# A hybrid decoder block on one core: the first query tile of the a heads in one matmul, the first weights cast by two engines, and fewer low parts on GpSimd

## The chip, the core and the metric

The kernel runs on one core of a Trainium2 chip. The metric is the device time of one execution in microseconds (us), less is better. Each time below is either the median of separate runs or comes from one profiled execution. The engines are named as in the profile: PE is TensorE's matmul stream and PEld its weight loads, DVE is VectorE, ACT is ScalarE, POOL is GpSimd, SP is the queue from which nearly all DMAs are issued.

## What is computed

The reference is one layer of a decoder block on 512 tokens of width 2048, in float32:

```python
h = _rms_norm(x, norm1_g[l])
proj = h @ w_in[l]
aq, ak, av, bu, bg, cq, ck, cv = jnp.split(proj, splits, axis=-1)
...
out_a = _dilated_mixture(aq, ak, av)        # 8 heads x 64, three dilated windows
out_b = _conformer_conv(bu, bg, ...)        # GLU, causal conv of 31 taps, LayerNorm, swish
out_c, _ = _band_attention(cq, ck, cv, C_WINDOW - 1, sinks=c_sinks[l])   # 16 heads, window 128
mix = jnp.concatenate([out_a, out_b, out_c], axis=-1)
x = x + mix @ w_out[l]
h2 = _rms_norm(x, norm2_g[l])
x = x + (jax.nn.silu(h2 @ w_gate[l]) * (h2 @ w_up[l])) @ w_down[l]
```

## The kernel before

**Precision.** Every float32 operand is held as a high part (`fp32r`, made by a cast on ACT) and a low part (what is left, made by a subtraction). A product is three matmuls: high with high, high with low, low with high. Helper `mm3` issues them (lines L312 to L314).

**Weights.** All weights come as units of 128x1024 numbers. `next_unit` hands the next one to PE, and ahead of that `split_up_to` splits units to come: `wh` is the high part, `wl` the low part. For the units of the input and output projections ACT casts (L289) and DVE subtracts (L290), both in SBUF. From a point behind the output projection on, ACT casts twice, once into a PSUM tile `wn` ("near") and once into SBUF (L293, L294), and DVE subtracts the PSUM copy (L295). That point is the number `len(units) + 4`: units 0 to 3 of the feed-forward part are still split in SBUF, and unit 4, called ('12', 'g1') in the profile, is the first with a near copy. Besides, POOL adds pairs of these units (L200), which the feed-forward part's seven products per block (as in Strassen's scheme) need.

**Stages.** First the head: `x` arrives in 16 tiles, each is scaled by the norm's weights (high part on ACT at L419, low part on DVE at L420) and multiplied for four column groups at once into the banks `in0` to `in3`; here the tokens are the stationary operand and 512 weights stream. Then `project` makes the other 26 column groups one by one, with attention work between their matmuls. Then come the output projection (banks `o`, L312 to L314 again), the gate and up projections (L1125, banks `out`) and the down projection (L1267, L1125).

**Order.** There is no scheduler on the chip: a table of "ticks" sets at which point in PE's stream each step of attention is recorded, and each engine executes its own list in that order, waiting on semaphores.

**Attention.** `attention` handles two heads at a time. `scores` multiplies one tile of 128 queries with the keys; the query holds its high part in 64 partitions and its low part in the other 64, so one matmul with the keys' high part `kh` and one with their low part `kl` give the whole product. `top` takes the row maximum with the mask added, `exps` the exponential, `norm` the sum and POOL's multiplication by its inverse (L779). `flip` transposes the weights on PE into a bank `t` (L795), ACT and DVE split them (`ph`, `pl`), and `weigh` multiplies by the values (bank `o`, L819 and L820). For the c heads the first query tile has 128 keys only; their high and low parts stand beside each other in a tile `k0`, one matmul of 256 columns meets both (L736), and `top` adds the two halves with a copy on ACT and an add on DVE (tile `kl`, L746 and L747). The a heads have two matmuls of 128 columns there (L738 and L739).

**Rows of the mix.** Each finished pair of heads is a row (`c0`, `a2`, ...) of the output projection's input. `split_mix` splits it: `mh` by ACT (L864), `ml` by POOL for c rows and by DVE for the others (L865). The output projection starts with `first_two`, which multiplies rows in the order c0, c1, c2, c4, c5, c3, c7, c6 for two column groups; `split_rows(k)` splits the rows from k on that are due.

Of the kernel before, what the change touches and what calls it, by code (L numbers as in the profile page):

```python
# [9 lines left out]
F32 = mybir.dt.float32  # L10
F32R = mybir.dt.float32r
# [4 lines left out]
P = 128  # L16
T = 512
NT = T // P
D = 2048
KT = D // P  # L20
# [28 lines left out]
ROWS = "c0 c1 c2 c4 c5 c3 c7 c6 a0 a1 b2 b1 b0 b3 a2 a3".split()  # L49
# [38 lines left out]
C_G1, C_G2, C_CW, C_CB, C_LG, C_LB, C_QK, C_SINK, C_ALL = 0, 16, 32, 156, 160, 164, 168, 172, 188  # L88
# [34 lines left out]
def kernel(ctx: ExitStack, tc: tile.TileContext, xT, wi, wo, wgu, wd, cst_in, outT):  # L123
    nc = tc.nc
# [20 lines left out]
    def slot(name, dt=F32, cols=T):  # L145
        return sp.tile([P, cols], dt, name=name, tag="s")
# [19 lines left out]
    raws, held = {}, {}  # L166
# [101 lines left out]
    splits = {}  # L268
# [11 lines left out]
    def split_up_to(i):  # L280
        while at["split"] <= min(i, len(works) - 1):
            key, last, eng = works[at["split"]]
            t, n = drop(key) if last else raws[key]
            u = at["split"]
            hi = wp.tile([P, 1024], F32R, name=f"wh{u}", tag="hi", bufs=SPLIT_BUFS)
            lo = wp.tile([P, 1024], F32R, name=f"wl{u}", tag="lo", bufs=SPLIT_BUFS)
            if eng or u < len(units) + 4:
                eng = eng or nc.vector
                nc.scalar.copy(hi[:, :n], t[:, :n])  # L289
                eng.tensor_sub(lo[:, :n], t[:, :n], hi[:, :n].bitcast(F32))  # L290
            else:
                near = psum["high"].tile([P, 1024], F32R, name=f"wn{u}", tag="h")
                nc.scalar.copy(near[:, :n], t[:, :n])  # L293
                nc.scalar.copy(hi[:, :n], t[:, :n])  # L294
                nc.vector.tensor_sub(lo[:, :n], t[:, :n], near[:, :n].bitcast(F32))  # L295
            splits[u] = (hi, lo)
            at["split"] += 1
# [13 lines left out]
    def mm3(out, wh, wl, xh, xl, start, stop):  # L311
        nc.tensor.matmul(out, wh, xh, start=start, stop=False)  # L312
        nc.tensor.matmul(out, wh, xl, start=False, stop=False)  # L313
        nc.tensor.matmul(out, wl, xh, start=False, stop=stop)  # L314
# [4 lines left out]
    xs = []  # L319
# [27 lines left out]
    def col(i):  # L347
        return cst[:, i:i + 1]
# [64 lines left out]
    def scaled(x, g, tag, k):  # L413
        if k < N_WIDE:
            both = wide(k, f"{tag}{k}", F32R)
            hi, lo = both[:, :T], both[:, T:]
        else:
            hi, lo = slot(f"{tag}h{k}", F32R), slot(f"{tag}l{k}", F32R)
        nc.scalar.activation(hi, x, AF.Copy, scale=g)  # L419
        nc.vector.scalar_tensor_tensor(lo, x, g, hi.bitcast(F32), op0=ALU.mult, op1=ALU.subtract)  # L420
        return hi, lo
# [19 lines left out]

    g4 = [(column if j < COLUMN_BANKS - 1 else bank)(f"in{j}") for j in range(HEAD4)]
    h_hl = {}
    for k in range(2):
        h_hl[k] = scaled(xs[k], col(C_G1 + k), "h", k)
        split_up_to(k)
    pump(RAW_EARLY)
    add_square(ssum, xs[0], 0, "sq")
    for k in range(KT):
        if k + 2 < KT:  # L450
            h_hl[k + 2] = scaled(xs[k + 2], col(C_G1 + k + 2), "h", k + 2)
        if k < 2 or k % 2 == 0:
            wh, wl = next_unit()
            o = 0
        if k + X_AHEAD < KT:
            load_first(k + X_AHEAD)
        if k == 4:
            nc.sync.dma_start(cst[:, C_G2:], cst_in[:, C_G2:])
        if k + 1 < KT:
            add_square(ssum, xs[k + 1], k + 1, "sq")  # L460
        hi, lo = h_hl.pop(k)
        h_hi.append(hi)
        h_lo.append(lo)
        for i in range(NT):
            s = slice(i * P, (i + 1) * P)
            mm3(g4[i], hi[:, s], lo[:, s], wh[:, o:o + T], wl[:, o:o + T], k == 0, k == KT - 1)
        o += T
    xs = None
    c64 = cp.tile([P, NT], F32, name="c64")
# [142 lines left out]
    def do_k(box, b, name, gi):  # L612
        def then(r):
            ticks.after(2, widen, r)

        raw = head_scales(b, name, then)
        box["k at"] = ticks.now + SQ + TD + 10
        both = []

        def widen(r):  # L620
            wide = slot(name + "wide")
            nc.scalar.copy(wide.rearrange("p (a b c) -> p a b c", a=NT, b=2),
                           r[:, :, :, None].to_broadcast([P, NT, 2, HD]))
            ticks.after(1, flip, wide)

        def flip(wide):
            b2 = bank(name + "t")
            for i in range(NT):
                nc.tensor.transpose(b2[:, i * P:(i + 1) * P], wide[:, i * P:(i + 1) * P], ident)
            ticks.after(1, scale, b2)  # L630

        def scale(b2):
            for h in range(2):
                both.append(slot(f"{name}{h}"))
                nc.vector.scalar_tensor_tensor(both[h][HALF[h]], raw[HALF[h]], gqk[HALF[h], gi:gi + 1], b2[HALF[h]],
                                               op0=ALU.mult, op1=ALU.mult)
            ticks.after(1, twin)

        def twin():
            for h in range(2):  # L640
                nc.sync.dma_start(both[h][HALF[1 - h]], both[h][HALF[h]])
            ticks.after(TD, high)

        def high():
            box["k"] = [(slot(f"{name}h{h}", F32R), slot(f"{name}l{h}", F32R)) for h in range(2)]
            for h in range(2):
                nc.scalar.copy(box["k"][h][0], both[h])
            ticks.after(1, low)

        def low():  # L650
            for h, (hi, lo) in enumerate(box["k"]):
                nc.vector.tensor_sub(lo, both[h], hi.bitcast(F32))
            if gi == 1:
                box["k0"] = [slot(f"{name}0{h}", F32R, 2 * P) for h in range(2)]
                for k0, src in zip(box["k0"], both):
                    nc.scalar.copy(k0[:, :P], src[:, :P])
                    nc.vector.tensor_sub(k0[:, P:], src[:, :P], k0[:, :P].bitcast(F32))
# [21 lines left out]
    def do_v(box, b, name):  # L679
# [22 lines left out]

    UNITS = {
        "c": [[(0, 0, 128, 0), (1, 0, 256, 256)], [(2, 128, 256, 0), (3, 256, 256, 256)]],
        "a": [[(0, 0, 128, 0), (1, 0, 256, 128)], [(2, 0, 384, 0)], [(3, 0, 512, 0)]],
    }

    TBANKS = {
# [6 lines left out]
    def attention(kind, box, mix, mi, heads):  # L715
# [7 lines left out]
        def head(h):  # L723
# [5 lines left out]
            def scores(u):  # L729
                q = box["q"][h]  # L730
                kh, kl = box["k"][h]
                b = banks[u] = bank(f"{name}s{h}{u}")
                for i, k0, n, o in us[u]:
                    qs, ks = slice(i * P, (i + 1) * P), slice(k0, k0 + n)
                    if kind == "c" and i == 0:
                        nc.tensor.matmul(b[:, o:o + 2 * n], q[:, qs], box["k0"][h], start=True, stop=True)  # L736
                        continue
                    nc.tensor.matmul(b[:, o:o + n], q[:, qs], kh[:, ks], start=True, stop=False)  # L738
                    nc.tensor.matmul(b[:, o:o + n], q[:, qs], kl[:, ks], start=False, stop=True)  # L739

            def top(u):
                b, rq = banks[u], box["rq"]
                s = slice(us[u][0][0], us[u][-1][0] + 1)
                if kind == "c" and u == 0:
                    with_kl = slot(f"kl{h}", F32, P)
                    nc.scalar.copy(with_kl, b[:, P:2 * P])  # L746
                    nc.vector.tensor_add(with_kl, with_kl, mask[:, mw - P:])  # L747
                for i, k0, n, o in reversed(us[u]):
                    other = with_kl if kind == "c" and i == 0 else mask[:, mw - n:]
                    nc.vector.tensor_tensor_reduce(b[:, o:o + n], b[:, o:o + n], other,  # L750
                                                   op0=ALU.add, op1=ALU.max, scale=1.0, scalar=-3.0e38,
                                                   accum_out=mx[:, i:i + 1])
                nc.vector.scalar_tensor_tensor(nm[:, s], mx[:, s], -1.0, rq[:, s, h], op0=ALU.mult, op1=ALU.mult)
                if kind == "c":
                    nc.vector.tensor_scalar(nm[:, s], nm[:, s], nsink[:, heads[h]:heads[h] + 1], None, op0=ALU.min)
# [104 lines left out]
    def split_mix(name):  # L860
        if name not in m_hi:
            m = mix.pop(name)
            hi, lo = slot(f"mh_{name}", F32R), slot(f"ml_{name}", F32R)
            nc.scalar.copy(hi, m)  # L864
            (nc.gpsimd if name[0] == "c" else nc.vector).tensor_sub(lo, m, hi.bitcast(F32))  # L865
            m_hi[name], m_lo[name] = hi, lo

    vd = tc.dram_tile([NT, P, T], F32, name="vd")
# [136 lines left out]
            operand(q, j, src)  # L1005

    def split_rows(k):
        for name in ROWS[k:k + 3]:
            if name in mix:
                split_mix(name)  # L1010

# [524 lines left out]
```

## Time and profile before

| what | value |
|---|---|
| median of 3 runs | 1879.63 us (1879.41 to 1881.6) |
| profiled execution, its own time | 1879.36 us |
| its span, first to last instruction | 1877.5 us |
| granted TensorE clock, mean over the span | 1.00 |
| busy share of PE, DVE, ACT, POOL | 100%, 77%, 72%, 65% |
| instructions of PE | 9848 matmuls, 9848 weight loads |

A row of the timeline reads: start in us, duration in us, engine, line of the kernel, operation, tile written, tiles read, shapes, count; in brackets the idle time of the engine before it and what ended that. A busy PE is not PE at its peak: matmuls overlap, and a matmul of 512 columns that is shown with 0.39 us starts 0.23 us after the one before it. So the cost of a matmul is read from start to start.

### The profile page before, as it was taken

How to read it: one execution, taken by the hardware profiler on the slowest of the kernel's cores; microseconds unless marked ns; L12 is line 12 of the kernel's file. 1: busy time of each engine (PE TensorE's matmuls, PEld its weight loads, DVE VectorE, ACT ScalarE, POOL GpSimd, SP SyncE). 2: the span in 40 equal slices, each digit the busy share in tenths (PEclk: the TensorE clock that was granted, in tenths of full speed). 3: DMA queues.
4: the chain of work that ended last, by engine and by line, in shares of the span. 5: the costliest groups of instructions: out<-in, count | busy, mean ns of one | idle time of the engine just before them, and what ended most of it. 6: DMA issues, size and time to landing. Idle time of an engine off the chain costs nothing.

```text
span 1877.5 us, 28557 instructions
## 1 busy us (share of the span) xinstructions
PE 1871.7 (100%) x9848; PEld 1609.1 (86%) x9848; DVE 1454.1 (77%) x2376; ACT 1343.7 (72%) x1883; POOL 1217.0 (65%) x812
## 2 busy tenths in 40 slices
PE   9999999999999999999999999999999999999999
PEld 7888888888888888888888888888888888888888
DVE  7578999897679777777777777777777677778887
ACT  6246655553466887888878888888888887777675
POOL 5023444362155887778878877888787767766786
PEclk9999999999999999999999999999999999999999
DMA  7333233333342354443544445344455475578984
GB/s 271 122 109 102 81 105 102 121 107 138 113 146 89 114 178 142 163 163 132 184 134 164 162 137 181 132 166 160 145 175 196 151 237 185 196 253 283 311 241 124
DMA packets 157986, 301.09 MB, mean 160 GB/s; under 512 B 29968, under 2 KB 69008, under 8 KB 157840
## 3 DMA queue, kind: packets, MB, share of 16 engines
q1 hardware_dynamic: 157696, 299.25, 48.8%
q8 instruction: 78, 1.28, 0.3%
q14 instruction: 68, 0.56, 0.1%
q10 hardware_dynamic: 144, 0.01, 0.0%
HBM read 241.27 MB, written 50.33 MB: 155 GB/s over the span
## 4 chain that ended last, share of the span: by engine, by line
PE 96%; DVE 1%; issue 1%; ACT 1%; POOL 1%; DMA 0%; SPq 0%; DVEq 0%; POOLq 0%; ACTq 0%
PE out L1125 51%; PE out L1267 16%; PE o L313 3%; PE o L314 3%; PE o L312 3%; PE cq L312 1%; PE cq L313 1%; PE cq L314 1%; PE in L313 1%; PE ak L312 1%; PE bg L312 1%; PE ak L314 1%; PE ak L313 1%; PE bu L312 1%; PE bu L314 1%; PE bg L313 1%
## 5 line engine op out<-in xcount | busy, mean ns | idle before, releaser
L1125 PE MATMUL out<-h,wh 128*128 128x512 f32 x2464 | 588.4, 391 | 0.0
L1125 PEld LDWEIGHTS out<-h,wh 128*128 128x128 f32 x2464 | 452.7, 188 | 87.5
L1125 PEld LDWEIGHTS out<-h,wl 128*128 128x128 f32 x2464 | 316.2, 191 | 12.4 <-DVE wl L295 0.4
L1125 PE MATMUL out<-h,wl 128*128 128x256 f32 x2464 | 320.3, 283 | 0.2 <-DVE wl L295 0.2
L1267 PE MATMUL out<-wh,a 128*128 128x512 f32 x896 | 221.3, 389 | 0.0
L1267 PEld LDWEIGHTS out<-wh,a 128*128 128x128 f32 x896 | 168.2, 188 | 34.9
L289 ACT CAST wh<-w 128x1024 fp32r<-128x1024 f32 (+1 forms) x93 | 96.7, 1042 | 125.0 <-PE o L313 43.3
L290 DVE TENSOR_TENSOR wl<-w,wh 128x1024 fp32r<-128x1024 f32 (+1 forms) x93 | 117.2, 1262 | 46.7 <-ACT wh L289 45.7
L1267 PE MATMUL out<-wl,a 128*128 128x512 f32 x448 | 119.7, 389 | 0.0
L1267 PEld LDWEIGHTS out<-wl,a 128*128 128x128 f32 x448 | 84.1, 188 | 17.4
L513 DVE SCALAR_TENSOR_TENSOR y<-bu,cst,y 128x511 f32<-128x511 f32 (+14 forms) x120 | 90.3, 753 | 0.7
L1125 PE MATMUL out<-a,wh 128*128 128x512 f32 x330 | 80.1, 391 | 0.0
L1125 PEld LDWEIGHTS out<-a,wh 128*128 128x128 f32 x330 | 60.2, 188 | 11.4
L312 PE MATMUL o<-mh_c,wh 128*128 128x512 f32 x128 | 51.2, 400 | 0.0
L313 PE MATMUL o<-ml_c,wh 128*128 128x512 f32 x128 | 50.1, 392 | 0.4 <-POOL ml_c L865 0.3
L314 PE MATMUL o<-mh_c,wl 128*128 128x512 f32 x128 | 50.1, 391 | 0.0
L1312 DVE TENSOR_TENSOR Y<-Y,out 128x512 f32<-128x512 f32 x48 | 30.8, 683 | 19.0 <-PE out L1267 18.9
L1125 PEld LDWEIGHTS out<-a,wl 128*128 128x128 f32 x330 | 43.3, 191 | 2.2
L1125 PE MATMUL out<-a,wl 128*128 128x256 f32 x330 | 44.0, 283 | 0.0
L429 POOL TENSOR_TENSOR ssum<-ssum,sq 128x512 f32<-128x512 f32 x15 | 26.6, 1770 | 19.3 <-ACT sq L428 18.8
L312 PE MATMUL cq<-hh,wh 128*128 128x512 f32 x96 | 38.6, 402 | 0.0
L314 PE MATMUL cq<-hh,wl 128*128 128x512 f32 x96 | 37.5, 391 | 0.0
(3111 smaller groups left out, 5197.0 us busy)
## 6 DMA issues: line engine op xcount, KB each, us to landing
od<-a SPq DMA_DIRECT2D x140, 256.0 KB, 4.7
a<-od SPq DMA_DIRECT2D x140, 256.0 KB, 6.2
w<-in_wi SPq DMA_DIRECT2D x59, 512.0 KB, 3.6
w<-in_wo SPq DMA_DIRECT2D x32, 512.0 KB, 3.6
x<-in_xT SPq DMA_DIRECT2D x16, 256.0 KB, 6.7
xr<-in_xT SPq DMA_DIRECT2D x16, 256.0 KB, 3.8
x2d<-xr SPq DMA_DIRECT2D x16, 256.0 KB, 2.0
yd<-z SPq DMA_DIRECT2D x16, 256.0 KB, 5.5
```

Of the source, the lines that this page charges most:

```text
L289: nc.scalar.copy(hi[:, :n], t[:, :n])
L290: eng.tensor_sub(lo[:, :n], t[:, :n], hi[:, :n].bitcast(F32))
L312: nc.tensor.matmul(out, wh, xh, start=start, stop=False)
L313: nc.tensor.matmul(out, wh, xl, start=False, stop=False)
L314: nc.tensor.matmul(out, wl, xh, start=False, stop=stop)
L429: eng.tensor_add(acc, acc, sq)
L513: nc.vector.scalar_tensor_tensor(yconv[j][:, i:], hconv[j][:, :T - i], c, yconv[j][:, i:], op0=ALU.mult, op1=ALU.add)
L1125: nc.tensor.matmul(out, lhs[:, s], rhs, start=begin, stop=last and low == flip[0] and x is xs[-1], skip_group_check=True)
L1267: nc.tensor.matmul(to[h], x[:, h * P:(h + 1) * P], v[:, j], start=sub == 0 and h not in started, stop=sub == 1 and n in (len(todo) - 1, le ...
L1312: nc.vector.tensor_add(t, t, b)
```

## The change

It has five parts, all in one diff.

1. **First weights.** DVE casts the first 128 columns of the very first weight unit and ACT the other 384; DVE subtracts afterwards over all 512. The twelve matmuls of the first `x` tile are recorded in another order: four of high with high, four of the low tokens, four of the low weights.
2. **One more unit split in SBUF.** The bound `len(units) + 4` is now `+ 5`, so that unit ('12', 'g1') has no near copy any more.
3. **The a heads' first query tile.** They get a `k0` tile as the c heads have it (two casts on ACT and two subtractions on DVE of 128 columns for each of the four key tiles), one matmul instead of two for each of the eight heads, and the copy and the add in `top`. The two 256-column tiles for a pair of heads now share one slot.
4. **Rows.** POOL makes the low parts of c4, c5 and c3 alone (`ROWS[3:6]`); those of c0, c1, c2, c7 and c6 go to DVE.
5. **Look-ahead.** `split_rows` looks at four rows instead of three.

```diff
-            if eng or u < len(units) + 4:
+            if u == 0:
+                nc.vector.tensor_copy(hi[:, :P], t[:, :P])
+            elif eng or u < len(units) + 5:
                 eng = eng or nc.vector
                 nc.scalar.copy(hi[:, :n], t[:, :n])
                 eng.tensor_sub(lo[:, :n], t[:, :n], hi[:, :n].bitcast(F32))
...
-    for k in range(2):
-        h_hl[k] = scaled(xs[k], col(C_G1 + k), "h", k)
-        split_up_to(k)
+    t0 = raws[0][0]
+    split_up_to(0)
+    h_hl[0] = scaled(xs[0], col(C_G1), "h", 0)
+    hi, lo = splits[0]
+    nc.scalar.copy(hi[:, P:T], t0[:, P:T])
+    nc.vector.tensor_sub(lo[:, :T], t0[:, :T], hi[:, :T].bitcast(F32))
+    t0 = None
+    h_hl[1] = scaled(xs[1], col(C_G1 + 1), "h", 1)
+    split_up_to(1)
...
+        if k == 0:
+            for x, w in ((hi, wh), (lo, wh), (hi, wl)):
+                for i in range(NT):
+                    nc.tensor.matmul(g4[i], x[:, i * P:(i + 1) * P], w[:, :T], start=x is hi and w is wh, stop=False)
+            continue
...
-            if gi == 1:
-                box["k0"] = [slot(f"{name}0{h}", F32R, 2 * P) for h in range(2)]
+            if True:
+                k0s = slot(f"{name}0", F32R)
+                box["k0"] = [k0s[:, :2 * P], k0s[:, 2 * P:]]
...
-        "a": [[(0, 0, 128, 0), (1, 0, 256, 128)], [(2, 0, 384, 0)], [(3, 0, 512, 0)]],
+        "a": [[(0, 0, 128, 0), (1, 0, 256, 256)], [(2, 0, 384, 0)], [(3, 0, 512, 0)]],
...
-                    if kind == "c" and i == 0:
+                    if i == 0:
                         nc.tensor.matmul(b[:, o:o + 2 * n], q[:, qs], box["k0"][h], start=True, stop=True)
...
-                if kind == "c" and u == 0:
+                if u == 0:
                     with_kl = slot(f"kl{h}", F32, P)
...
-            (nc.gpsimd if name[0] == "c" else nc.vector).tensor_sub(lo, m, hi.bitcast(F32))
+            (nc.gpsimd if name in ROWS[3:6] else nc.vector).tensor_sub(lo, m, hi.bitcast(F32))
...
-        for name in ROWS[k:k + 3]:
+        for name in ROWS[k:k + 4]:
```

Three places of the instruction lists show what moves. The first is PE at the start of the head, where `in` are the four banks, `wh` and `wl` the first weight unit and `h` the scaled tokens (high and low part share one tile). Before:

```order
L312 MATMUL in_139<-wh_146,h_143 128x512
L313 MATMUL in_139<-wl_147,h_143 128x512
L314 MATMUL in_139<-wh_146,h_143 128x512
L312 MATMUL in_140<-wh_146,h_143 128x512
L313 MATMUL in_140<-wl_147,h_143 128x512
L314 MATMUL in_140<-wh_146,h_143 128x512
```

The same place with the change:

```order
L475 MATMUL in_139<-wh_143,h_146 128x512
L475 MATMUL in_140<-wh_143,h_146 128x512
L475 MATMUL in_141<-wh_143,h_146 128x512
L475 MATMUL in_142<-wh_143,h_146 128x512
L475 MATMUL in_139<-wh_143,h_146 128x512
L475 MATMUL in_140<-wh_143,h_146 128x512
L475 MATMUL in_141<-wh_143,h_146 128x512
L475 MATMUL in_142<-wh_143,h_146 128x512
L475 MATMUL in_139<-wl_144,h_146 128x512
```

The low weights `wl`, which stood second, now stand ninth.

The second place is DVE ahead of the output projection, during the last input column group; `a1e` are weights of head pair a1, `a1pl` their low parts after the transposition, `ak3v` the square sums of the last key tile, `a2s` scores of pair a2. Before:

```order
L513 SCALAR_TENSOR_TENSOR y_3318<-bu_3092,cst,y_3318 128x489
L775 SCALAR_TENSOR_TENSOR a1e_4020,a1d_3612<-a1e_4020,mult_a 128x384
L777 RECIPROCAL a1d_3612<-a1d_3612 128x1
L806 TENSOR_TENSOR a1pl_4053<-a1t_3985,a1ph_4026 128x512
L578 TENSOR_REDUCE ak3v<-ak3sq 128x8
L580 TENSOR_TENSOR ak3v<-ak3v,c_524 128x8
L750 ISA a2s_4042,a2d_3780<-a2s_4042,bias_a 128x256
```

The same place with the change:

```order
L526 SCALAR_TENSOR_TENSOR y_3332<-bu_3104,cst,y_3332 128x489
L879 TENSOR_TENSOR ml_c_4046<-mix_c_1387,mh_c_4045 128x512
L789 SCALAR_TENSOR_TENSOR a1e_4043,a1d_3626<-a1e_4043,mult_a 128x384
L791 RECIPROCAL a1d_3626<-a1d_3626 128x1
L879 TENSOR_TENSOR ml_c_4070<-mix_c_1975,mh_c_4069 128x512
L820 TENSOR_TENSOR a1pl_4075<-a1t_4008,a1ph_4049 128x512
L591 TENSOR_REDUCE ak3v<-ak3sq 128x8
L593 TENSOR_TENSOR ak3v<-ak3v,c_525 128x8
L761 TENSOR_TENSOR kl_4088<-kl_4088,bias_a 128x128
L764 ISA a2s_4065,a2d_3798<-a2s_4065,bias_a 128x256
```

Two low parts of c rows and the add of the a head have come in; a third low part (c2) follows 15 rows further on, and two (c7, c6) behind that. They are gone from POOL's list, where the three that stay now follow each other.

The third place is DVE at the start of the feed-forward part; `out` are its banks, `n2s` the second norm's sums. Before:

```order
L438 TENSOR_SCALAR n2v<-n2s 128x4
L1133 TENSOR_REDUCE g1r<-out_5955 128x256
L1138 TENSOR_TENSOR g1r<-g1r,out_5953 128x256
L1139 TENSOR_TENSOR g1r<-g1r,out_5953 128x256
L295 TENSOR_TENSOR wl_6086<-w('12', 'g1')_5686,wn_6087 128x1024
L295 TENSOR_TENSOR wl_6092<-w('22', 'g1')_5538,wn_6093 128x1024
```

The same place with the change:

```order
L440 TENSOR_SCALAR n2v<-n2s 128x4
L1147 TENSOR_REDUCE g1r<-out_5991 128x256
L1152 TENSOR_TENSOR g1r<-g1r,out_5989 128x256
L1153 TENSOR_TENSOR g1r<-g1r,out_5989 128x256
L292 TENSOR_TENSOR wl_6122<-w('12', 'g1')_5722,wh_6121 128x1024
L297 TENSOR_TENSOR wl_6126<-w('22', 'g1')_5574,wn_6127 128x1024
```

The order is the same; the first of the two subtractions now reads both operands from SBUF (`wh`) instead of one from PSUM (`wn`).

More of the change, by code (lines that the diff above doesn't have):

```diff
@@ L463 @@
         h_lo.append(lo)
+        if k == 0:
[3 more added lines that the diff above has]
+            continue
         for i in range(NT):
             s = slice(i * P, (i + 1) * P)
[L466 removed]
+            mm3(g4[i], hi[:, s], lo[:, s], wh[:, o:o + T], wl[:, o:o + T], False, k == KT - 1)
         o += T
@@ L748, in top @@
                 for i, k0, n, o in reversed(us[u]):
-                    other = with_kl if kind == "c" and i == 0 else mask[:, mw - n:]
+                    other = with_kl if i == 0 else mask[:, mw - n:]
                     nc.vector.tensor_tensor_reduce(b[:, o:o + n], b[:, o:o + n], other,
```

## The prediction, made before the changed kernel ran

> **What bounds the kernel now.** I read the page first, then the list of waits of PE's weight loads, then the timeline around each of these waits, engine by engine. From the page, the chain that ended last, and from the waits of PEld (waiter, line, what it waited for, us in total, times, longest):
>
> ```profile
> PE 96%; DVE 1%; issue 1%; ACT 1%; POOL 1%; DMA 0%; SPq 0%; DVEq 0%; POOLq 0%; ACTq 0%
> PEld o L313 <- POOL ml_c L865: 1.1, 2, 0.7
> PEld in L313 <- DVE wl L290: 1.1, 3, 0.5
> PEld a1t L795 <- PE o L314: 0.5, 1, 0.5
> PEld out L1125 <- DVE wl L295: 0.4, 1, 0.4
> ```
>
> TensorE is the path: 96% of the chain, and what it waits for in mid-stream adds up to some 3 us of 1877.5. So a change can gain in two ways only: fewer instructions on PE, or one of these short waits gone. And it can lose wherever a helper now comes later than PE does. Each part is costed by that.
>
> **Part 1, the first weights.** The start of the head, PEld with ACT and DVE:
>
> ```profile
> 5.99 0.19 PEld L313 LDWEIGHTS in<-wl,h 128*128 128x128 f32 x1 [0.54 <-DVE wl L290]
> 6.67 0.73 ACT L419 ACTIVATE h<-x,cst 128x512 fp32r<-128x512 f32 x1 [1.46 <-DMA x<-in_xT]
> 8.11 0.69 DVE L290 TENSOR_TENSOR wl<-w,wh 128x512 fp32r<-128x512 f32 x1
> 8.85 0.19 PEld L313 LDWEIGHTS in<-wl,h 128*128 128x128 f32 x1 [0.23 <-DVE wl L290]
> 9.40 1.05 ACT L289 CAST wh<-w 128x1024 fp32r<-128x1024 f32 x1 [0.18 <-DMA w<-in_wi]
> 10.48 1.22 DVE L290 TENSOR_TENSOR wl<-w,wh 128x1024 fp32r<-128x1024 f32 x1 [0.48 <-ACT wh L289]
> 11.76 0.19 PEld L313 LDWEIGHTS in<-wl,h 128*128 128x128 f32 x1 [0.31 <-DVE wl L290]
> ```
>
> The 0.54 us before 5.99 go: the low weights now stand ninth, some 2 us later. But two later waits take their place. The second `x` tile's matmuls wait for low weights that are ready at 8.80 (8.11 + 0.69), in a chain that begins with ACT waiting for the DMA of that tile until 6.67. The third's wait until 11.70 (10.48 + 1.22), behind a cast that waits for a weight DMA until 9.40. The change touches neither DMA. Today PE goes on at 11.76 and it will again, whatever it saves before. DVE's new cast of 128 columns (at most the 0.28 us of the add below) delays the first low tokens, which are not needed until the fifth matmul. I take 0; the bounds are 0.06 gained (11.76 to 11.70) and, if a restart costs what it does elsewhere, 0.1 lost.
>
> **Part 2, the a heads' first tile.** Weight loads of the scores of an a head (after a transposition, up to the next projection's load), then of a c head, which already has the form that the a heads get:
>
> ```profile
> 393.99 0.19 PEld L738 LDWEIGHTS a2s<-ak2h,aq 128*128 128x128 f32 x1
> 394.10 0.19 PEld L739 LDWEIGHTS a2s<-ak2l,aq 128*128 128x128 f32 x1
> ...
> 394.44 0.19 PEld L312 LDWEIGHTS aq<-hh,wh 128*128 128x128 f32 x1
> ...
> 136.77 0.19 PEld L736 LDWEIGHTS c3s<-ck,cq 128*128 128x128 f32 x1
> ...
> 137.12 0.19 PEld L312 LDWEIGHTS bg<-hh,wh 128*128 128x128 f32 x1
> ```
>
> The a head takes 0.45 us for four matmuls, the c head 0.35 for three. Each small matmul costs the 0.11 us of its weight load, however few columns stream. Eight heads save 8 x 0.11 = 0.9 us. [...]
>
> Around it ACT gets 8 copies and 8 casts, DVE 8 adds and 8 subtractions of 128 columns. They lie beside matmuls, since DVE is free for a quarter of the span, except around 400 us, where DVE is the busy one. That is the next part.
>
> **Part 3, the rows' low parts, and part 5, the look-ahead.** The start of the output projection, PE first, then POOL and DVE; the group row gives the cost of an add of 128 columns:
>
> ```profile
> 403.07 0.19 PEld L313 LDWEIGHTS o<-ml_c,wh 128*128 128x128 f32 x1 [0.44 <-POOL ml_c L865]
> 405.95 0.39 PE L314 MATMUL o<-mh_c,wl 128*128 128x512 f32 x1
> 406.45 0.42 PEld L795 LDWEIGHTS a1t<-ident,a1e 128*128 128x128 f32 x4 [0.53 <-PE o L314]
> 413.25 0.19 PEld L313 LDWEIGHTS o<-ml_c,wh 128*128 128x128 f32 x1 [0.66 <-POOL ml_c L865]
> 399.08 1.22 DVE L290 TENSOR_TENSOR wl<-w,wh 128x1024 fp32r<-128x1024 f32 x1
> 401.63 4.43 POOL L865 TENSOR_TENSOR ml_c<-mix_c,mh_c 128x512 fp32r<-128x512 f32 x3
> 392.93 1.68 DVE L775 SCALAR_TENSOR_TENSOR a1e<-a1e,mult_a 128x384 f32<-128x384 f32 x1
> 401.44 0.43 DVE L775 SCALAR_TENSOR_TENSOR a2e<-a2e,mult_a 128x256 f32<-128x256 f32 x1 [0.16 <-ACT a2e L763]
> 402.31 0.70 DVE L750 CUSTOM_DVE_ANT_0 a2s<-a2s,bias_a 128x512 f32<-128x512 f32 x1 [0.24 <-PE a2s L739]
> 403.10 1.19 DVE L753 SCALAR_TENSOR_TENSOR a2d<-a2d,aq2r 128x1 f32<-128x1 f32 x1
> 404.81 1.52 DVE L635 SCALAR_TENSOR_TENSOR ak<-ak3raw,gqk,ak3t 64x512 f32<-64x512 f32 x2
> 407.76 0.54 DVE L775 SCALAR_TENSOR_TENSOR a2e<-a2e,mult_a 128x384 f32<-128x384 f32 x1
> 413.14 0.68 DVE L865 TENSOR_TENSOR ml_a<-mix_a,mh_a 128x512 fp32r<-128x512 f32 x1
> 413.74 0.68 DVE L775 SCALAR_TENSOR_TENSOR a2e<-a2e,mult_a 128x512 f32<-128x512 f32 x1
> L747 DVE TENSOR_TENSOR kl<-kl,bias_c 128x128 f32<-128x128 f32 x16 | 4.5, 280 | 1.0 <-ACT kl L746 1.0
> ```
>
> The two waits for POOL (403.07 and 413.25, 1.1 us together) go. Row c2's low part was third in POOL's list. It will stand behind DVE's subtraction at 399.08, which ends at 400.3 today and 0.3 us later with what changes ahead of it (two low parts and an add in, 1.14 us out, below); with its own 0.6 us it is there at 401.2. PE, which now waits 0.44 us for it until 403.07, wants it at 402.5. Row c6's was last on POOL and has 4 us to spare on DVE.
>
> But PE also waits at 406.45, and this wait is one for DVE, though the row names PE: the transposition's bank is the one that DVE's two L635 read until 406.33 (404.81 + 1.52). A matmul of 512 columns starts 0.23 us after the one before, so PE, without the wait, would be there at 405.95 + 0.23 = 406.18: it costs 0.3 us now. What of DVE's list changes ahead of L635? Added: three low parts (c0, c1, c2) at 0.60 us from start to start (413.14 to 413.74), and one add of 0.28: 2.1 us. Gone: 1.14 us of the instruction at 392.93, which took 1.68 instead of the 0.54 of its twin at 407.76 because POOL's first low part ran beside it. Absorbed: DVE's idle 0.16 and 0.24. Left: +0.55, so L635 ends near 406.9 and PE goes on near 407.0. PE itself is there earlier, at 406.18 - 0.5 (no wait at 403.07) - 0.1 (one weight load) = 405.6. The new wait is 1.4 us.
>
> Sum here: -1.1 - 0.3 + 1.4 = 0. The bounds: DVE's 1.19 us at 403.10 (an instruction on 4 numbers per head, otherwise 0.16) is again a wait for POOL's row of three, which stays as it is. If it goes as well, the new wait is 0.2 and the part gains 1.2; if a second of DVE's instructions meets POOL in the same way, it costs 1.2 more. I stand in the middle, where one such wait stays, as today. The other two low parts and `ml_a0` come behind L635 and have 4 us before PE wants them.
>
> **Part 4, one more unit split in SBUF.** The start of the feed-forward part, and first an older place where the same two instructions met:
>
> ```profile
> 577.98 2.41 POOL L200 TENSOR_TENSOR w('21', 'g1')_5483<-w('21', 'g1')_5483,w('11', 'g1')_5585 128x1024 f32<-128x1024 f32 x1
> 578.07 3.39 DVE L290 TENSOR_TENSOR wl<-w,wh 128x1024 fp32r<-128x1024 f32 x1
> ...
> 605.00 2.40 POOL L200 TENSOR_TENSOR w('s', 'g1')_5737<-w('s', 'g1')_5737,w('12', 'g1')_5686 128x1024 f32<-128x1024 f32 x1
> 605.35 1.21 DVE L295 TENSOR_TENSOR wl<-w('12', 'g1')_5686,wn 128x1024 fp32r<-128x1024 f32 x1
> 607.35 2.41 POOL L200 TENSOR_TENSOR w('s', 'u1')_6078<-w('21', 'u1')_5991,w('22', 'u1')_5993 128x1024 f32<-128x1024 f32 x1
> 607.65 1.22 DVE L295 TENSOR_TENSOR wl<-w('22', 'g1')_5538,wn 128x1024 fp32r<-128x1024 f32 x1 [1.08 <-ACT wn L293]
> 607.65 1.11 PE L1125 MATMUL out<-h,wl 128*128 128x256 f32 x8
> 608.92 0.19 PEld L1125 LDWEIGHTS out<-h,wl 128*128 128x128 f32 x1 [0.36 <-DVE wl L295]
> ```
>
> What it means to do: ACT saves one cast, the near copy of unit '22' no longer waits for unit '12', and PE's wait of 0.4 us at 608.92 goes. What I expect: the subtraction of unit '12' changes from L295 (one operand in PSUM) to L290 (both in SBUF). At 605.35 POOL's addition, 0.35 us old, did not disturb the L295. At 578.07 an L290, 0.09 us behind an addition, took 3.39 us instead of 1.2: it ended at 581.46, 1.07 us after the addition did. So here the low part of '12' is ready at 605.00 + 2.40 + 1.07 = 608.47 instead of 606.56. PE wants it at 607.65 and waits 0.9 us. Its eight matmuls (1.1 us) end at 609.6, and the next eight, which start at 608.92 today, follow there: unit '22' is ready by then too (608.4 + 1.2). Loss: 609.64 - 608.92 = 0.7 us, today's wait already taken off. Before this point DVE works without a break and in PE's pace, so gains from earlier are kept.
>
> **The sum.** Against the profiled execution: 1879.36 + 0 (first weights) - 0.9 (scores) + 0 (rows) + 0.7 (unit '12') = 1879.2 us. The median of the runs is 0.27 above the profiled execution, so I forecast 1879.4 us: no change. Differences under 0.2% (3.8 us) are about what a measurement of this kernel can't tell from no change.
>
> **Rivals.**
> - *Everything gained.* DVE gets its turn before POOL at 605 and at 403: -0.9, -1.2 and -0.4, 1877.1 us. For it: POOL's three low parts may start later now, behind DVE. Against: POOL's 0.35 us lead at 605 hangs on work that the change does not move. 20%.
> - *GpSimd keeps its turn.* Where POOL's instructions follow each other, DVE got in between in the rows above (at 403.10 it was over at 404.29, within the three). If it does not, DVE waits for all of them: at 605 for the second addition too (until 609.76), so that PE's second eight start at 609.76 + 1.07 + 1.1 = 611.9, 3.0 us late and not 0.7; at 403 until 406.06 and not 404.29, 1.8 us. 1879.4 + 2.3 + 1.8 = 1883.5 us, slower. It decides if POOL's list has no gap when DVE arrives. Only the rows against it speak: 6%.
> - *The merged matmul saves nothing.* If a small matmul costs by its columns and not by its weight load, one of 256 takes as long as two of 128: 1879.4 + 0.9 = 1880.3 us. Against it the c heads' rows: 7%. [...]
> - *The opening pays.* If the DMAs land earlier than in this profile, the 0.5 us before 5.99 are real: 1878.9 us. 7%.
>
> The forecast itself has 55%; 5% stay for what I don't see, such as slots for tiles that come free later because four more are held. These cases lie nearly all within 0.2%: 0.91; slower 0.06 (the second rival and part of the unseen), faster 0.03. The range reaches from the first rival to the sum with a second meeting of DVE and POOL (1.2) and the runs' own spread upwards (1881.6 against 1879.63): 1877.0 to 1881.8.
>
> **What would show it.** In the changed profile: the weight load behind the third `x` tile's low weights again at about 11.76; seven or eight 0.11 us steps gone from the a heads' scores; no wait of `o` for `ml_c`, and instead a wait of over 1 us before the second transposition of pair a1, with DVE's L635 ending just ahead; and one DVE subtraction of unit ('12', 'g1') of over 3 us, with POOL's addition under it. The forecast is wrong if that subtraction takes 1.2 us, if PE has no wait near 406, or if waits of the weight loads appear elsewhere, above all between 420 and 576 us.

## The result, and the profile after

The changed kernel takes 1882.29 us (median of 20 runs, 1881.50 to 1883.57), the kernel before 1879.26 us (20 runs): the ratio is 1.0016, with a 95% interval of 1.0010 to 1.0021. It is slower, by 3.0 us where I had forecast a difference of nothing, and 0.5 us above the range. (Three of the runs that this document reports, one of norm_act and two of the kernel before, took over 2300 us at a mean granted clock of 0.68 to 0.75 and are left out of all medians.) The profiled execution took 1881.54 us (span 1879.8), 0.75 us less than its median; the kernel before's took 1879.36. This 0.75 is a part of the answer, as the clock shows below.

The chain that ended last, then the waits of PEld and of PE (waiter, line, what it waited for, us in total, times, longest):

```profile
PE 96%; DVE 3%; issue 0%; ACT 0%; DMA 0%; SPq 0%; DVEq 0%; ACTq 0%
...
PEld a1t L809 <- issue: 3.2, 1, 3.2
...
PEld out L1139 <- DVE wl L292: 1.1, 1, 1.1
...
PEld a1t L809 <- POOL a1e L793: 0.4, 1, 0.4
PEld a0s L750 <- PE c4t L809: 0.3, 1, 0.3
...
PE a1t L809 <- DVE ak L648: 2.8, 1, 2.8
```

DVE's share of the chain has gone from 1% to 3%, and the 1% each of POOL, ACT and issue is gone: behind the new wait the chain follows DVE's list, from 377.9 us to 408.6. The waits of `o` for `ml_c` (1.1 us) are gone, as meant. In their place stands one wait before the second transposition of pair a1, this time of PE itself for DVE's `ak`: 2.8 us. The place in the timeline of PE, DVE and POOL (L648, L767, L789, L292, L879, L793 are the L635, L753, L775, L290, L865, L779 of before):

```profile
405.59 0.40 PE L316 MATMUL o<-mh_c,wl 128*128 128x512 f32 x1
408.74 0.63 PE L809 MATMUL a1t<-ident,a1e 128*128 128x128 f32 x4 [2.76 <-DVE ak L648]
...
391.72 1.23 DVE L292 TENSOR_TENSOR wl<-w,wh 128x1024 fp32r<-128x1024 f32 x1
394.26 0.55 DVE L789 SCALAR_TENSOR_TENSOR a1e<-a1e,mult_a 128x384 f32<-128x384 f32 x1
401.03 1.10 DVE L879 TENSOR_TENSOR ml_c<-mix_c,mh_c 128x512 fp32r<-128x512 f32 x1
402.70 1.06 DVE L767 SCALAR_TENSOR_TENSOR a2d<-a2d,aq2r 128x1 f32<-128x1 f32 x1
403.89 1.50 DVE L789 SCALAR_TENSOR_TENSOR a2e<-a2e,mult_a 128x256 f32<-128x256 f32 x1
407.08 1.52 DVE L648 SCALAR_TENSOR_TENSOR ak<-ak3raw,gqk,ak3t 64x512 f32<-64x512 f32 x2
...
402.45 4.09 POOL L879 TENSOR_TENSOR ml_c<-mix_c,mh_c 128x512 fp32r<-128x512 f32 x3
```

PE is done at 405.6 + 0.23 and goes on at 408.74; L648 ends at 408.60, not at 406.9 as I had it. Read DVE's durations: the 256-column L789 takes 1.50 us where the same form took 0.43 before (401.44), the L767 takes 1.06 where 0.16 is usual (1.19 before, so this meeting stayed, as expected). Both lie under POOL's row of three. The 0.55 at 394.26 is the stall that went.

The second loss is where it was expected, DVE and POOL at the start of the feed-forward part:

```profile
606.83 3.12 DVE L292 TENSOR_TENSOR wl<-w('12', 'g1')_5722,wh 128x1024 fp32r<-128x1024 f32 x1
609.87 1.21 DVE L297 TENSOR_TENSOR wl<-w('22', 'g1')_5574,wn 128x1024 fp32r<-128x1024 f32 x1
...
606.48 2.39 POOL L200 TENSOR_TENSOR w('s', 'g1')_5773<-w('s', 'g1')_5773,w('12', 'g1')_5722 128x1024 f32<-128x1024 f32 x1
```

If each of PE's matmuls is set against the same matmul before, the lateness is +0.06 us at 402.5, -0.24 at 402.8 (the wait for `ml_c2` is gone), +2.26 behind the wait at 408.7, +1.4 to 1.5 from 430 on (the wait for `ml_c6` is gone and the merges go on saving), +2.35 at unit '12', +2.2 at the end. With the 0.75 us between the profiled execution and the median, and the 0.1 us by which the kernel before's profile lies on the other side, these are the 3.0 us.

### The profile page after: what moved, and what is told of

The parts are those of the page before. It is cut to its first block, busy times and chain, and to the rows that moved or that the text cites. A ratio compares the mean times of both kernels' runs of the same rounds, so it can differ in the third digit from the quotient of the medians.

```text
span 1879.8 us, 28573 instructions
## 1 busy us (share of the span) xinstructions
PE 1870.4 (100%) x9840; PEld 1608.2 (86%) x9840; DVE 1461.0 (78%) x2398; ACT 1345.9 (72%) x1898; POOL 1211.2 (64%) x807
## 3 DMA queue, kind: packets, MB, share of 16 engines
q8 instruction: 78, 1.28, 0.3%
## 4 chain that ended last, share of the span: by engine, by line
PE 96%; DVE 3%; issue 0%; ACT 0%; DMA 0%; SPq 0%; DVEq 0%; ACTq 0%
PE out L1139 51%; PE out L1281 16%; PE o L314 3%; PE o L316 3%; PE o L315 3%; PE cq L314 1%; PE cq L315 1%; PE cq L316 1%; PE bg L314 1%; PE bu L314 1%; PE bg L315 1%; PE bu L316 1%; PE bg L316 1%; PE bu L315 1%; DVE wl L292 1%; PE in L316 1%
## 5 line engine op out<-in xcount | busy, mean ns | idle before, releaser
L292 DVE TENSOR_TENSOR wl<-w,wh 128x1024 fp32r<-128x1024 f32 (+1 forms) x92 | 117.0, 1273 | 45.9 <-ACT wh L291 45.6
```

## The experiments

Times are medians of 11 runs (ten for norm_act), ratios to the kernel before with their 95% interval. Those intervals are about 0.09% (1.7 us) to each side, so differences under that are read from the traces and from kernels that ran side by side.

### Which edit costs: each taken back alone

**no_plus5** (the changed kernel with):

```diff
-            elif eng or u < len(units) + 5:
+            elif eng or u < len(units) + 4:
```

> The changed kernel, with unit ('12', 'g1') split through PSUM again. Theory A, from the two traces: POOL's addition at 607.5 us holds up the one subtraction that now reads two SBUF operands, and PE stands 0.9 us later from there to the end. Then PE's wait at that unit is 0.4 us again, the subtraction takes 1.2 us, and the time is 0.7 to 0.9 us under the changed kernel's 1882.3: about 1881.5. Theory B: the end of the kernel is set by something else and absorbs this: 1882.3.

1882.01 us, 1.0014 [1.0005, 1.0023]. PE's lateness no longer steps at unit '12': it is 2.9 us before and behind it, and the subtraction takes 1.22 us. The median fell by 0.3 only, since more of its runs had the low clock shown below (7 of 11, the changed kernel 10 of 20); its runs at full clock have a median of 1880.95, the changed kernel's 1881.78.

**rows_back**:

```diff
-            (nc.gpsimd if name in ROWS[3:6] else nc.vector).tensor_sub(lo, m, hi.bitcast(F32))
+            (nc.gpsimd if name[0] == "c" else nc.vector).tensor_sub(lo, m, hi.bitcast(F32))
...
-        for name in ROWS[k:k + 4]:
+        for name in ROWS[k:k + 3]:
```

> The changed kernel, with all c rows' low parts on POOL again and split_rows looking at three rows. Theory A: the new wait of 2.8 us before the second transposition of pair a1 comes from the three low parts on DVE; with them back on POOL it falls to 0.3 to 0.6 us (0.28 of it is the add that the scores' merge brings), the waits of the output projection for ml_c return (1.1 us): net 1.4 to 1.8 us less, 1880.5 to 1880.9. Theory B: the wait comes from the add and the copies that the scores' merge puts on DVE and ACT there: then it stays above 2 us, the ml_c waits come on top, and the time is 1883.

1880.80 us, 1.0008 [0.9999, 1.0017]: theory A. The waits of `o` for `ml_c` are back, but larger than in the kernel before (2.2 us against 1.1), and the long wait is gone.

**scores_back** (`UNITS["a"]`, the `k0` tiles, `scores` and `top` as before: two matmuls of 128 columns for an a head's first query tile).

> The changed kernel, with the a heads' first query tile in two matmuls again. Theory A: the merge saves 8 times 0.11 us, of which new small waits (0.24 at a0s, 0.33 at a1t, 0.1 at a1s) eat 0.6, and it puts one add of 0.28 us in front of the late L648: without it the time is within 0.3 us of the changed kernel's: 1882.0 to 1882.6. Theory B: the merge itself is what costs (more copies on ACT and DVE delay the a heads): 1 us or more faster than the changed kernel, under 1881.3. If the savings are whole: 1883.2.

1882.87 us, 1.0018 [1.0009, 1.0026]. The long wait stays (2.5 us of PE), so the merge is not what makes it. At full clock its three runs have 1881.4, the changed kernel's ten 1881.78, against a hope of 0.9 saved: the merge pays nothing.

**opening_back** (the first weights and matmuls as before).

> The changed kernel, with the first weights and the first matmuls as in the kernel before. Theory A: the opening is decided by the x and w DMAs and the later low weights, so nothing changes: 1882.2 to 1882.4. Theory B: the opening costs something in most runs that the one profiled execution (1881.54, among the lowest of 20 runs) does not show, since the changed kernel's median lies 0.75 us above its profile and its runs scatter over 2 us where those of the kernel before scatter over 0.6: then the time falls by 0.5 to 0.8 us to 1881.6 and the scatter with it.

1883.30 us, 1.0020 [1.0011, 1.0029]: Theory B falls, the opening costs nothing, and the scatter is wider (1881.77 to 1884.75). The profiled execution, the slowest of them, showed where the scatter comes from. Windows of PE's timeline (length, PE busy, granted clock, DMA):

```profile
406.00:408.00 2.00, 0.26 (x2) 1.00 0.00 0
408.00:410.00 2.00, 0.95 (x5) 0.57 0.67 143
410.00:412.00 2.00, 2.00 (x8) 0.50 0.95 204
412.00:414.00 2.00, 2.00 (x8) 0.50 0.72 243
414.00:416.00 2.00, 2.00 (x9) 0.73 0.01 4
```

Behind the wait the granted clock is at half, for 6.8 us (0.86 x 2 + 2 + 2 + 0.54 x 2). In the profile of no_plus5, at the same clock, a matmul of 512 columns starts 0.43 us after the one before (410.94, 411.37) instead of 0.23. In the profiled execution of the changed kernel, as in ten of its 20 runs, the clock stayed at 1.00: matmuls of 512 columns start 0.23 us apart right behind the wait (409.88, 410.10, 410.33).

### What makes the wait

**pool_rows_out**:

```diff
-            hi, lo = slot(f"mh_{name}", F32R), slot(f"ml_{name}", F32R)
+            hi = slot(f"mh_{name}", F32R)
             nc.scalar.copy(hi, m)
-            (nc.gpsimd if name in ROWS[3:6] else nc.vector).tensor_sub(lo, m, hi.bitcast(F32))
+            if name in ROWS[3:6]:
+                lo = m_lo[ROWS[0]]
+            else:
+                lo = slot(f"ml_{name}", F32R)
+                nc.vector.tensor_sub(lo, m, hi.bitcast(F32))
```

> The changed kernel, in which POOL's three low parts (c4, c5, c3) are left out and c0's low part stands for them. DVE's instruction list is the same. Theory A: three of DVE's instructions ahead of L648 stand still while POOL's row of three runs (L767 1.06 us, L789 with 256 columns 1.50, and c2's low part 1.10 behind POOL's 400 us instruction, where 0.26, 0.42 and 0.68 are their usual durations): without it the first two give back 1.9 us, PE's wait before the second transposition of a1 falls from 2.8 to about 0.9 us, and the clock stays at 1.0: 1879.3 to 1880.0, with little scatter. Theory B: DVE is late because its own list is longer by three low parts and an add: the wait stays at 2.5 to 2.8 us and the time at 1881.5 to 1882.3.

1879.52 us, 0.9999 [0.9990, 1.0009], runs from 1879.22 to 1880.09: theory A, 2.8 us gone without a change in DVE's list. DVE:

```profile
401.31 1.10 DVE L883 TENSOR_TENSOR ml_c<-mix_c,mh_c 128x512 fp32r<-128x512 f32 x1
402.98 0.16 DVE L767 SCALAR_TENSOR_TENSOR a2d<-a2d,aq2r 128x1 f32<-128x1 f32 x1
403.27 0.42 DVE L789 SCALAR_TENSOR_TENSOR a2e<-a2e,mult_a 128x256 f32<-128x256 f32 x1
405.26 1.52 DVE L648 SCALAR_TENSOR_TENSOR ak<-ak3raw,gqk,ak3t 64x512 f32<-64x512 f32 x2
```

1.06 became 0.16 and 1.50 became 0.42: 2.0 us that DVE had stood still for POOL's row. Of PE's gap of 3.15 us from start to start 1.07 are left. That c2's low part still takes 1.10 us shows that its extra 0.4 is not from the row.

**c2_c6_dve** (opening and merge, the rest as before, but two low parts on DVE):

```diff
-            (nc.gpsimd if name[0] == "c" else nc.vector).tensor_sub(lo, m, hi.bitcast(F32))
+            (nc.gpsimd if name[0] == "c" and name not in ("c2", "c6") else nc.vector).tensor_sub(lo, m, hi.bitcast(F32))
```

> Only the opening, the merge of the a heads' first tile, and two low parts (c2, c6) on DVE instead of five; look-ahead of three rows and unit ('12', 'g1') through PSUM as in the kernel before. Theory A: the merge's savings stay (about 0.6 net), the wait for ml_c6 goes (0.7), the wait for ml_c2 goes (0.6 to 1.3) but c2's low part and the add put 0.9 us into DVE's list ahead of L648, so the wait before the second transposition of a1 is about 1.2 instead of 0.3: net 0.6 + 0.7 + 0.6 - 0.9 = 1.0 under the kernel before, 1878.3. Theory B: each shift of DVE's list makes it meet POOL's row of three in another place and costs another us: 1879.3 or more.

1882.30 us, 1.0013 [1.0004, 1.0022]: my arithmetic was off by 4 us. With c0 and c1 on POOL again and only c2's low part put ahead of L648, DVE meets the row at the same places for the same time:

```profile
402.95 1.05 DVE L767 SCALAR_TENSOR_TENSOR a2d<-a2d,aq2r 128x1 f32<-128x1 f32 x1
404.13 1.50 DVE L789 SCALAR_TENSOR_TENSOR a2e<-a2e,mult_a 128x256 f32<-128x256 f32 x1
```

So what counts here is not how many low parts DVE has, but where these two instructions stand against POOL's row. In rows_back and scores_only the same L789 is over at 402.4, before the row begins, and takes 0.42.

### The clock

**warm_fill** (in the first two output columns, behind row c4) and **half_fill** (the same for one of the two columns, three matmuls):

```diff
                 mm3(b, wh[:, s], wl[:, s], m_hi[row], m_lo[row], k == 0, k == 7)
+            if k == 3:
+                for b, wh, wl in two:
+                    mm3(b, wh[:, s], wl[:, s], m_hi[row], m_lo[row], False, False)
             ticks.tick()
```

> The changed kernel, in which the six matmuls of row c4 run twice (so that row counts double in two output columns): 1.4 us of work for PE inside its 2.8 us wait before the second transposition of a1. Theory A: the wait of 2.8 us lets the granted clock fall to 0.5 for 3 us or more in most executions (three of four profiles), which is the 0.75 us by which the median lies above the unthrottled profile. With a wait of 1.4 us the clock stays at 1.0: although PE has more to do, the median falls to 1881.3 to 1881.7 and the runs scatter over less than 0.8 us. Theory B: the clock has nothing to do with it and the scatter comes from elsewhere (the opening, DMAs): median 1882.3 and a scatter of 2 us, as before.

1881.93 us, 1.0013 [1.0004, 1.0022]. All 11 runs have a mean clock of 1.0 and scatter over 0.9 us, though the median is 0.2 above what I had expected.

> The changed kernel, in which three matmuls of row c4 (the first of the two output columns) run twice, 0.7 us of work inside the wait before the second transposition of a1: from start to start some 2.4 us are left, where the changed kernel has 3.15 and warm_fill 1.8. If the clock falls after about 2 us without a matmul, some of the runs show a mean clock of 0.999 and the runs scatter over 1.5 to 2 us as those of the changed kernel do. If it needs about 3 us, all runs show 1.0, the scatter is under 1 us and the median 1881.7, as with warm_fill.

1883.17 us, 1.0018 [1.0009, 1.0027]; seven of 11 runs have a mean clock of 0.999, which in the profiled runs means such a stretch at half clock, and a median of 1883.43, the four others 1881.75. One of the seven was profiled. PE's wait, and windows as above:

```profile
PE a1t L809 <- DVE ak L648: 2.1, 1, 2.1
...
408.00:409.00 1.00, 0.36 (x4) 1.00 0.76 166
409.00:410.00 1.00, 1.00 (x8) 0.70 0.94 199
410.00:411.00 1.00, 1.00 (x4) 0.50 0.98 215
411.00:412.00 1.00, 1.00 (x4) 0.50 0.93 225
412.00:413.00 1.00, 1.00 (x7) 0.60 1.00 340
413.00:414.00 1.00, 1.00 (x7) 1.00 0.10 35
```

Over all kernels, by PE's longest wait: 1.4 to 1.6 us, none of 22 runs with a low clock (warm_fill, one_row_later); 2.1 us, 7 of 11; 2.5 to 2.8 us, 42 of 64 (the changed kernel 10 of 20). The price, from the changed kernel's own runs: median 1882.93 with, 1881.78 without, 1.15 us (1.15 to 1.7 in the five other kernels that have both). The low clock lasts 3.4 us (0.6 + 1 + 1 + 0.8 above) or, in opening_back, twice that.

The windows of the five traces with a low clock say more. The clock fell at 408.40 us in no_plus5, 409.34 in scores_back, 408.28 in opening_back, 408.36 in c2_c6_dve and 409.40 in half_fill, and stayed at 0.50 for 3.40 to 3.42 us in four of them. In the 3.4 us just before the fall PE was busy for 1.0 to 1.4 us; in warm_fill and one_row_later it was busy for at least 1.7 of any 3.4 us around these waits, and the clock stayed up. Whether the length of the wait or PE's work around it sets the clock is not shown, nor what decides between the runs of one kernel: of the executions that had a wait of 2 us or more and kept the clock one was profiled, that of the changed kernel, and there PE was busy for only 0.65 us from 405.6 to 409.0.

### Can the wait be moved away?

**one_row_later**:

```diff
-            ticks.tick()
+            if k != 3:
+                ticks.tick()
```

> The changed kernel, with the ticks of the output projection's first two columns held for one row after row c4, so that PE has row c5's six matmuls (1.4 us) ahead of the second transposition of a1. Theory A: the wait shrinks from 2.8 to 1.4 us and the clock stays up: 1.4 us plus the 0.75 us of the clock less than 1882.3, so 1880.1 (to 1880.5 if what hangs on the ticks makes a later row wait). Theory B: the wait only moves, since all that follows the transposition comes a row later too: 1881.5 to 1882.3.

1882.60 us, 1.0018 [1.0009, 1.0027], all at full clock: theory B. The wait is 1.4 us, as meant, but a new one stands where the layer norm, a tick later too, is late:

```profile
PE lnm L547 <- DVE part L545: 1.6, 1, 1.6
...
PE a1t L809 <- DVE ak L648: 1.4, 1, 1.4
```

**norm_act** (c6_dve, below, and):

```diff
+                    if name == "a1" and h == 1 and u == 2:
+                        ticks.after(1, lambda x, r: nc.scalar.activation(x, x, AF.Copy, scale=r), e[:, o:o + n], rd[:, i:i + 1])
+                    else:
-                    nc.gpsimd.tensor_scalar(e[:, o:o + n], e[:, o:o + n], rd[:, i:i + 1], None, op0=ALU.mult)
+                        nc.gpsimd.tensor_scalar(e[:, o:o + n], e[:, o:o + n], rd[:, i:i + 1], None, op0=ALU.mult)
```

> c6_dve, and in pair a1's second head the normalisation of the 512-column tile goes from POOL (2.6 us at 400) to ACT (one ACTIVATE, some 0.7 us, a tick later). POOL's row of three low parts then starts at 399.9 instead of 402.45. Theory A: the wait for ml_c2 (1.3 us from start to start where 0.23 is usual, in rows_back) goes; and since DVE meets the row earlier, one of its instructions (the split at 399.9, or L767) still stands still for about 1 us, as in the kernel before: 0.7 to 1.1 under c6_dve, 1878.0 to 1878.4. Theory B: POOL's list was not what c2 waits for, or two or more of DVE's instructions meet the row now: 1879 or more.

1880.94 us, 1.0006 [0.9997, 1.0016]: theory B's second half. The wait for `ml_c2` goes, and POOL's earlier row meets two other instructions of DVE, which take 1.22 and 1.55 us in rows_back:

```profile
399.67 2.31 DVE L292 TENSOR_TENSOR wl<-w,wh 128x1024 fp32r<-128x1024 f32 x1
...
406.94 2.87 DVE L688 TENSOR_TENSOR av<-av3s,av 128x256 fp32r<-128x256 f32 x2
```

### What the parts are worth without the long wait

**scores_only** (the kernel before with the merge alone).

> The kernel before with the a heads' merge alone. By weight loads (0.11 us for each small matmul): 0.9 saved; against that an add of 0.28 us more on DVE ahead of L648, which PE waits for at 406 already, and the waits of 0.24 at a0s and 0.33 at a1t that all kernels with the merge show: net 0 to 0.4 saved, 1878.9 to 1879.3. If the new order puts DVE or POOL another us late around 400 us (as two low parts did in the last runs): 1880 or more. By streamed columns alone (nothing saved): 1879.6 to 1880.

1879.94 us, 1.0001 [0.9991, 1.0010]; beside it the kernel before had 1879.46. The merge gives back what it saves, and not where I looked:

```profile
PEld o L313 <- POOL ml_c L866: 2.2, 3, 1.1
```

In the kernel before this is 1.1 us. DVE is late ahead of 386 us: its split of a weight unit stands at 385.96 where it stood at 385.30, and from there to 406 DVE has hardly a pause, so POOL's normalisations, which wait for DVE, and behind them its row of low parts start 0.8 us later (402.41 for 401.63), while PE is there at the same time (402.44 for 402.46). Of what makes DVE late, the a heads' subtractions and adds since 368 us are 0.7 us, and 0.84 us come in one step, from ACT:

```profile
375.92 0.91 ACT L764 ACTIVATE a1e<-a1s,a1d,aq1r 128x128 f32<-128x128 f32 x2 [3.43 <-PE a1s L739]
377.80 1.23 DVE L290 TENSOR_TENSOR wl<-w,wh 128x1024 fp32r<-128x1024 f32 x1 [0.84 <-ACT wh L289]
```

In the kernel before these stand at 372.41 and 376.76. ACT's exponentials of pair a1 wait 3.4 us, ACT's cast of a weight unit stands behind them, and DVE waits for the cast. The same is seen at this place in the changed kernel, rows_back, opening_back and c2_c6_dve, and not in scores_back or c6_open, which have no merge. Why ACT waits there is open.

**open_scores** (rows_back, and `+ 4` for `+ 5`).

> The changed kernel with the rows and unit ('12', 'g1') as in the kernel before; beside rows_back (1880.8, its clock at 1.0 throughout) it differs only in that unit, so it measures that edit without the clock's noise. Theory A (the meeting of POOL's addition with a subtraction that reads two SBUF operands): rows_back lost 0.9 to 1.1 us there, so 1879.8. Theory B (absorbed later): 1880.8.

1880.08 us, 1.0001 [0.9992, 1.0010], all at full clock. Rows_back lies 1.54 us above the kernel before that ran beside it, open_scores 0.62, and the two lie 0.72 apart: unit '12' costs 0.7 to 0.9 us. Theory A.

**c6_dve** (open_scores, with only c6 excepted from POOL: `name != "c6"`).

> open_scores with one row's low part (c6, the last on POOL) on DVE. It stands after L648, in DVE's free time, so the wait of the output projection for ml_c6 (0.68 us in the kernel before, 0.80 in rows_back) goes and nothing comes: 0.7 under open_scores, 1879.1. If it makes DVE meet POOL again, as c2's low part did ahead of L648, no gain: 1879.8 or more.

1879.74 us, 1.0000 [0.9991, 1.0008], 0.34 us under open_scores, half of what I expected. The wait for `ml_c6` is gone, but DVE's low part of c6 (409.59, 1.14 us for 0.68) and POOL's of c7 (410.14, 1.74 us where open_scores has 1.29) run beside each other and both take longer, and PE waits for c7.

**c6_open** (c6_dve without the merge).

> The kernel before with the changed opening and c6's low part on DVE, without the merge of the a heads' first tile. If the merge is what lengthens the wait for ml_c2 from 0.61 to 1.3 us (POOL's row of three starts 0.8 us later in all kernels with it), this kernel keeps the kernel before's waits at 402 and 406, and loses only that for ml_c6 (0.68 to 0.23 from start to start): 0.4 to 0.7 us faster than the kernel before, 1878.6 to 1878.9. If c6 on DVE or the opening delay something too: 1879.3 or more.

1878.97 us, 0.9997 [0.9988, 1.0006]; runs from 1878.52 to 1879.17, the kernel before beside it at 1879.22. The wait for c2 is 0.60 us from start to start, as before (it is 1.28 with the merge), and PE gains 0.33 us at `ml_c6`. It is the best of the fourteen, but 0.25 us is not a difference that the interval tells from none.

## Why the prediction was wrong

**Opening: 0, held.** The 0.54 us wait behind the first low weights is gone. PE stood, behind the third `x` tile's low weights, 0.3 us earlier in this execution, and 0.04 to 0.8 earlier in the other kernels with the new opening, and 0.4 earlier in scores_only, which has the old one. The cast behind the weight DMA started at 8.91 here and at 8.72 in scores_only, where the kernel before had 9.40: the landing of the first DMAs decides, as said.

**Scores: -0.9, right in the step and wrong in the sum: +0.1.** An a head's scores went from 0.45 to 0.35 us, three weight loads for four, 0.11 us for each small matmul (in the kernel before even the eight of one column, `n2s`, have their weight loads from 601.57 to 602.47, 0.11 us apart):

```profile
394.13 0.19 PEld L750 LDWEIGHTS a2s<-ak,aq 128*128 128x128 f32 x1
...
394.48 0.19 PEld L314 LDWEIGHTS aq<-hh,wh 128*128 128x128 f32 x1
```

But at 402.5 us, with five of the eight heads merged, PE is 0.06 us late, though the opening had brought it 0.3 to the good: new waits of 0.3 (`a0s`, at 300 us) and 0.4 (`a1t` for POOL, at 390) and smaller ones took more than the five heads saved. The three heads behind give 0.3, and scores_only gained nothing. "They lie beside matmuls, since DVE is free for a quarter of the span, except around 400 us" was the fault: with the merge DVE is 0.75 us late at 386 us (386.05 for 385.30), and since it has hardly a pause from there on, it is still 0.8 late at 399.9.

**Rows: this step failed: +1.6 instead of 0.** The mechanism was the one I gave, PE waiting for L648 before the second transposition of a1. The size was not: 1.4 us were predicted, 2.9 came (3.15 from start to start). By PE's lateness the two waits that went gave 0.4 and 0.6, and the one that came took 2.6. I had L648 later by 0.55 us; it is later by 2.27. Of the 1.7 between, 0.75 is that DVE starts this stretch late (its split at 391.72 stood at 390.97 before), which comes with the merge, 1.08 is a second meeting with POOL's row (L789, 1.50 for 0.42), and 0.4 is c2's low part, 1.10 for 0.68; some 0.5 of this was made up, 0.3 of it by two L767 that took less than before. "One such wait stays, as today" was a guess in the middle between no meeting and two; the upper end was the right one, and pool_rows_out shows that it was the meeting.

**The clock: not in the prediction at all.** I priced a wait by its length. With its wait of 2.8 us the changed kernel took another 1.15 us in half of its runs, and five other kernels, with waits of 2.1 to 2.8 us, took another 1.15 to 1.7 us in seven to nine of 11. This price is a consequence of the wait that the rows had too small, and it carried the result over the range's upper end: at full clock the median, 1881.78, lies just inside.

**Unit '12': +0.7, right.** POOL's addition had a lead of 0.35 us again, the subtraction ended 1.08 us after it (1.07 predicted), PE's lateness grew by 0.89 and then fell to 0.75.

**Rivals.** "Everything gained" fell at both places. "GpSimd keeps its turn" has the nearest time (1883.5) but not the mechanism: DVE got in between POOL's instructions at 403.7 and at 608.87, and it met them one by one. "The merged matmul saves nothing" is refuted as a mechanism (0.35 against 0.45) though not in what the time shows. "The opening pays" came true in part: the DMAs landed earlier, and 0.3 us stayed.

## What to carry to other kernels

Where two engines hold each other up, a step that is moved changes which of their instructions meet; cost it by laying the two lists beside each other at the new times, and take the number of meetings as unknown. An engine that is busy without a pause passes every addition on (DVE, 0.75 us late at 386 us, was still 0.8 late at 399.9), so look for its idle time in the stretch before the wait and not in the span. And a wait of TensorE can have a price beyond its length: here 49 of 75 runs with a wait of 2.1 to 2.8 us had a lower mean clock, which cost 1.15 to 1.7 us, and none of 22 with one of 1.4 to 1.6 us.

## What the runs showed of the hardware that was not expected

- With a wait of PE of 2.1 to 2.8 us, 49 of 75 runs had a lower mean clock, and the five of them that were profiled show a granted clock of 0.5 for 3.40 to 3.42 us, in opening_back for 6.8 us. It did not always fall in the wait: in half_fill PE had worked for 0.76 us at full clock by then (408.64 to 409.40), in scores_back for 1.2 us (408.15 to 409.34). With waits of 1.4 to 1.6 us none of 22 runs showed it.
- Two DVE instructions that read two operands from SBUF and met a `TENSOR_TENSOR` of POOL ended with it or a little later: L767, on one number per row, took 1.06 us where 0.16 is usual (it ended at 403.76, POOL's first low part at 403.74), and the split of unit '12' took 3.12 us where 1.22 is usual and ended 1.08 us after POOL's addition. Behind POOL's `TENSOR_SCALAR` of 399.83 the split of 399.90 took its usual 1.22 us, but c2's low part, the next, 1.10 instead of 0.68. Why these two differ stays open.
